# One zero-filled product for the edge values of two query tiles, and two longer times in the planner of an encoder layer

## The chip, the cores and the metric

The kernel runs on one core of a Trainium2 chip. The metric is the device time of one launch in microseconds, the median of three runs. The profile is of one further execution of the same program.

## The reference

A hybrid encoder layer over 1024 positions of 1024 channels, in float32, with weights drawn at random:

```
h = LN1(alpha*x + 0.5*SwiGLU_a(x))
h = LN2(alpha*h + HybridMixer(h))
h = LN3(alpha*h + 0.5*SwiGLU_b(h))
```

Each SwiGLU has 2752 hidden channels. The mixer projects the input to queries, keys and values of 12 heads, to four Fourier groups and to gates. The part that the change touches most is the attention: three groups of four heads, with dilations 1, 4 and 16. A query at place i of its (strided) sequence attends to the keys from i - 64 to i + 64 of it; the sequence of a residue has 1024, 256 or 64 places. The scores get a relative bias, then softmax; the three groups of a head slot are combined by their softmax denominators.

## The kernel before, in words

**Products.** Nearly all products run on TensorE as three single-pass products of "parts": each operand is split into a rounded high part (a copy on ACT, `split.hi`) and the rest (a subtraction on DVE, `split.lo`). Matrix products are made by a seven-product (Strassen-like) scheme; one such product of a pair of column blocks is a job of 12 matmuls of 512 columns at L495. The attention products are plain float32: scores (L1592), transposition of the probabilities (`pt`, L1637) and values (`pv`, L1653). One float32 matmul stands in the trace as two records.

**Stages in order.** First feed-forward layer ("a"): gate and up products, then down products (tiles `qa...`). Values of all heads (`v`). Then 22 column pairs (u, q, s): each "q" pair is queries and keys of one head, and the attention of that head is put between the pair products that follow. Then the two projections of the mixer, the output product, and the second feed-forward layer ("b"; its down products' tiles are `qb...`). Residual, norms and stores go along.

**What sets the order.** A planner in the program (class `Flow`) simulates the engines while it emits instructions. PE has a fixed list of jobs, and "floats" (the attention products) that are emitted between jobs as soon as the planner believes their inputs are ready. Work of DVE (`V`), ACT (`S`) and GpSimd (`G`) is a node with a cost, its predecessors and a due time; each engine's clock in the plan takes the ready node with the earliest due time. Loads (`Q`) are issued on SP when they come due and when a page is free. A predecessor may carry a wait: `(q, 1.5)` means 1.5 us after the plan's end of `q`. In the plan a load ends 2.5 us after its bytes. What is emitted runs in that order on the chip; there each engine waits, in order, for what an instruction really needs, so a wrong time in the plan shows as an engine that stands.

**Buffers.** 46 pages of 128x1024, 11 halves of 128x512 (`NS2`), 8 PSUM banks. A node takes and gives back pages, halves (`halves=`, `hgives=`) and banks in the plan. `fl.later(n, us, hgives=2)` gives two halves back `us` after node `n`, which is how a plan waits for a store: the store itself is a DMA whose end the plan doesn't know.

**An attention step** (`one`, inside `attention`, L1563). Scores go to a bank; DVE adds the bias into a half `p` (L1606) and takes the maxima (L1616); ACT makes the exponentials (L1621); PE transposes `p` in slices of 128 keys (L1637); ACT copies that to a half `pT` (L1642); PE multiplies the values with it (L1653); ACT copies the result to the page `pv` (L1666 to L1671). Two query tiles are a step. For tiles in the middle of a sequence each has 256 keys, two full slices. At the ends of a sequence a tile has 192 keys: 128, and 64 more. The 64 of the two tiles share one slice: keys of the first tile in its rows 0 to 63, keys of the second in rows 64 to 127. There are 20 such steps, one in each head of group 0 and four in each head of group 1. Their list of products is

```python
where = [(qa, ka, P, 0, 0), (qb_, kb_ + 64, P, 0, 1), (qa, ka + P, 64, 0, 2), (qb_, kb_, 64, 64, 2)]
```

(query tile, first key, keys, first row, slice): two products over 128 keys and two over 64, each tile into a bank of its own. `load_values` (L1530) has loaded the values so that the 64 edge rows of both tiles lie above one another in one 128-row slice of its page, under two keys of the table `vf`.

**Weight parts that are stored early** (`keep_halves`, L1807). The output product's operands are cut into parts well ahead, while the values and the head pairs are computed, and kept in DRAM: a half is loaded, copied (L1820) and subtracted (L1824) into two halves, and these are stored by GpSimd's queue (L338) to `wob..._d` or `wot..._d`. There are 28 such pieces; the two halves are given back 6 us after the store's node.

**Down products** (`ffn`, L657). For each of seven products and eleven steps a page `q...` is loaded by SP with two DMAs (L849) and then split on ACT (L358) and DVE (L363). In stage "b" the last product is done by row tile, and its `qb` weight pages are loaded and split in `load_b4`'s loop. After its hidden columns stage "b" ends a pair with ACT copies `t2`, `t3` (L633), a subtraction `t3b` (L718) and further DVE work.

## Time and profile before

| what | us |
|---|---|
| median of 3 runs | 2058.83 |
| lowest, highest | 2058.13, 2060.5 |
| the profiled execution's own time | 2060.76 |
| its span, first to last instruction | 2059.0 |

| engine | busy us | share | instructions |
|---|---|---|---|
| TensorE, products | 2044.1 | 99% | 9451 |
| VectorE | 1333.7 | 65% | 1890 |
| ScalarE | 886.0 | 43% | 1395 |
| GpSimd | 267.5 | 13% | 464 |

The mean granted clock of TensorE was 0.998 of 2.4 GHz. The DMA engines moved 442 MB, 215 GB/s on average. How to read the trace: PE is the product pipe of TensorE, PEld its weight loads, DVE VectorE, ACT ScalarE, POOL GpSimd, SP the engine that issues most DMAs (a trailing q is an engine's queue). L1653 is a line of the program. Matmuls overlap, so the time from one start to the next is the rate, not the length that stands beside it. "[5.69 <-DMA x]" is idle time before an instruction and what ended it.

### The profile page before, as it was taken

The page shows a single profiled execution, that of the slowest core. Times are in us where ns is not written, and L with a number is a line of the kernel's source. Part 1 is how long each engine was busy: PE and PEld are TensorE (multiplying, and loading weights), DVE is VectorE, ACT ScalarE, POOL GpSimd, SP SyncE. Part 2 cuts the span into 40 slices and gives each one's busy share as a digit, 9 for nine tenths or more (in the row PEclk, how much of TensorE's full clock was granted, in tenths as well). Part 3 has the DMA queues.
Part 4 walks back from the last instruction along what each step waited for, and adds up shares of the span by engine and source line. Part 5 has one row for each costly group of instructions (what it writes and reads, how often), then busy time and mean ns, then how long its engine had stood idle before and what let it go on. Part 6 is the DMA issues. An engine that isn't in the chain of part 4 may idle for free.

```text
span 2059.0 us, 25821 instructions
## 1 busy us (share of the span) xinstructions
PE 2044.1 (99%) x9451; PEld 1701.3 (83%) x9451; DVE 1333.7 (65%) x1890; ACT 886.0 (43%) x1395; POOL 267.5 (13%) x464
## 2 busy tenths in 40 slices
PE   9999999999999999999999999999999999999998
PEld 7888888888888888878888888888888888888886
DVE  7765555577585668555656564687876665575565
ACT  6333333454453324555555443235633333355342
POOL 0122111011001122232122110000011101010000
PEclk9999999999999999999999999999999999999999
DMA  5778875599866558986777669584245433358753
GB/s 205 238 235 259 257 225 157 172 340 404 270 208 186 169 206 270 299 235 191 239 197 192 228 224 347 196 307 174 75 156 182 156 133 128 123 192 292 246 173 104
DMA packets 164144, 442.23 MB, mean 215 GB/s; under 512 B 20370, under 2 KB 42722, under 8 KB 163504
## 3 DMA queue, kind: packets, MB, share of 16 engines
q1 hardware_dynamic: 118928, 288.41, 40.9%
q0 software_dynamic: 45088, 152.16, 24.7%
q8 instruction: 74, 1.21, 0.2%
q14 instruction: 54, 0.44, 0.1%
HBM read 329.63 MB, written 176.91 MB: 246 GB/s over the span
## 4 chain that ended last, share of the span: by engine, by line
PE 96%; DMA 1%; issue 1%; DVE 0%; POOL 0%; ACT 0%; SPq 0%; DVEq 0%; POOLq 0%; ACTq 0%
PE Ab L495 13%; PE Aa L495 13%; PE Aq L495 7%; PE Da L495 6%; PE Db L495 5%; PE As L495 5%; PE Dq L495 3%; PE Xa L864 3%; PE Zb L864 3%; PE Xb L864 3%; PE Za L864 3%; PE pj L2110 2%; PE v L1291 2%; PE Ds L495 2%; PE wA L2199 2%; PE pv L1653 2%
## 5 line engine op out<-in xcount | busy, mean ns | idle before, releaser
L1621 ACT ACTIVATE p<-p,stat 128x192 f32<-128x192 f32 (+2 forms) x96 | 42.2, 441 | 25.6 <-DVE stat L1616 25.3
L338 POOL DMA_DIRECT2D hsaa<-t2a x21 | 12.0, 571 | 315.0 <-DVE t2a L730 296.9
L338 POOL DMA_DIRECT2D n_spill<-y x16 | 9.0, 566 | 297.8 <-DVE y L1061 297.8
L338 POOL DMA_DIRECT2D hsba<-t2b x21 | 11.4, 543 | 273.6 <-DVE t2b L730 273.6
L726 DVE TENSOR_TENSOR t2a<-Da,t2a 128x512 f32<-128x512 f32 x21 | 14.5, 692 | 45.2 <-PE Da L495 45.2
L1653 PEld LDWEIGHTS pv<-pT,v 128*128 128x128 f32 (+1 forms) x320 | 37.4, 189 | 5.2
L1653 PE MATMUL pv<-pT,v 128*128 128x128 f32 (+1 forms) x320 | 40.7, 288 | 0.0
L633 ACT ACTIVATE t2a<-Aa 128x512 f32<-128x512 f32 x21 | 12.6, 600 | 64.9 <-PE Aa L495 64.9
L1411 DVE SCALAR_TENSOR_TENSOR oq<-Dq,b_cols,t2q 128x512 f32<-128x512 f32 x12 | 11.8, 984 | 44.1 <-PE Dq L495 44.1
L1606 DVE SCALAR_TENSOR_TENSOR p<-sc,bias 128x512 f32<-128x512 f32 (+1 forms) x40 | 24.6, 620 | 24.2 <-PE sc L1592 14.4
L633 ACT ACTIVATE t2b<-Ab 128x512 f32<-128x512 f32 x21 | 12.6, 600 | 63.8 <-PE Ab L495 63.8
L726 DVE TENSOR_TENSOR t2b<-Db,t2b 128x512 f32<-128x512 f32 x21 | 14.5, 691 | 39.0 <-PE Db L495 39.0
L1592 PE MATMUL sc<-oq,oq 128*128 128x192 f32 (+2 forms) x192 | 35.4, 331 | 0.0
L718 DVE TENSOR_TENSOR t3a<-Da,t3a 128x512 f32<-128x512 f32 x21 | 14.5, 690 | 29.2 <-PE Da L495 26.7
L1592 PEld LDWEIGHTS sc<-oq,oq 128*128 128x128 f32 x192 | 31.0, 196 | 2.2
L495 PE MATMUL Db<-Zs40h,usb 128*128 128x512 f32 x84 | 29.4, 391 | 1.1 <-DVE t3b L718 1.1
L495 PE MATMUL Db<-Zs41h,usb 128*128 128x512 f32 x84 | 29.3, 389 | 0.0
L495 PE MATMUL Da<-Xs40h,usa 128*128 128x512 f32 x84 | 29.3, 389 | 0.0
L495 PE MATMUL Da<-Xs41h,usa 128*128 128x512 f32 x84 | 29.3, 389 | 0.0
L1411 DVE SCALAR_TENSOR_TENSOR oq<-Dq,b_cols,t3q 128x512 f32<-128x512 f32 x12 | 11.9, 992 | 26.8 <-PE Dq L495 24.6
L718 DVE TENSOR_TENSOR t3b<-Db,t3b 128x512 f32<-128x512 f32 x21 | 14.5, 690 | 21.9 <-PE Db L495 20.4
L1616 DVE TENSOR_REDUCE stat<-p 128x2 f32<-128x384 f32 (+2 forms) x40 | 24.2, 618 | 1.0
(7475 smaller groups left out, 7270.8 us busy)
## 6 DMA issues: line engine op xcount, KB each, us to landing
qa<-hsas SPq DMA_DIRECT2D x43, 256.0 KB, 5.8
qa<-tdat SPq DMA_DIRECT2D x43, 256.0 KB, 5.4
qb<-hsbs SPq DMA_DIRECT2D x43, 256.0 KB, 4.4
ga<-in_ffn_gu_dram SPq DMA_DIRECT2D x21, 512.0 KB, 5.9
ua<-in_ffn_gu_dram SPq DMA_DIRECT2D x21, 512.0 KB, 8.4
gb<-in_ffn_gu_dram SPq DMA_DIRECT2D x21, 512.0 KB, 3.6
ub<-in_ffn_gu_dram SPq DMA_DIRECT2D x21, 512.0 KB, 4.5
qb<-tdbt SPq DMA_DIRECT2D x33, 256.0 KB, 4.8
```

Source lines behind the costliest of these rows:

```text
L338: nc.gpsimd.dma_start(*a, **kw)
L495: nc.tensor.matmul(out, pick(w, a)[:, k * P:(k + 1) * P], self.cols(xn, b, k), start=first and k == 0 and ti == 0, stop=last and k == 3 an ...
L633: nc.scalar.activation(H[c, t], B[c, "B"], AF.Copy)
L718: nc.vector.tensor_sub(H[c, "t3"], B[c, "D"], H[c, "t3"])
L726: nc.vector.tensor_sub(H[c, "t2"], B.pop((c, "D")), H[c, "t2"])
L864: nc.tensor.matmul(bank_, a, b, start=first and ti == 0, stop=last and ti == len(todo) - 1, skip_group_check=True)
L1291: nc.tensor.matmul(ps, X2.cols(f"a{hf + 1}{k // 4 + 1}", a, k % 4)[:, mm * P:(mm + 1) * P], pick(wv, b), start=(k == 0 and ti == 0), stop= ...
L1592: nc.tensor.matmul(sv[:, i, :], qk[0][:, qt * P:(qt + 1) * P], qk[1][:, k0:k0 + w], start=True, stop=True, skip_group_check=True)
L1621: nc.scalar.activation(p3()[:, i, :], p3()[:, i, :], AF.Exp, bias=stats[h][:, k, 0:1], scale=1.0, accum_out=stats[h][:, k, 1:2])
L1653: nc.tensor.matmul(out_of(tiles.index(qt)), env["v"][kc, rows], pt[r0:r0 + rows, sl * P:(sl + 1) * P], start=qt not in seen, stop=last, sk ...
L2110: nc.tensor.matmul(bk[hf], pick(wv, a)[:, k, cc * P:(cc + 1) * P], pick(attn[k], b)[:, hf * 512:(hf + 1) * 512], start=(k == 0 and ti == 0 ...
L2199: nc.tensor.matmul(B["w", bk, m], X4.cols(xn, a, k)[:, m * P:(m + 1) * P], pick(w, b), start=new and k == 0 and ti == 0, stop=k == 3 and t ...
```

## The change

- `load_values`: the two 64-row entries become one entry "edge" for the full 128-row slice.
- `turned`: for steps of 192 keys the shared slice is copied into two slices: rows 0 to 63 into the one of the first tile, rows 64 to 127 into the other's. A new DVE node `blank` clears the other 64 rows of each. `values`: the edge keys of both tiles are one product of 256 columns over 128 rows, half of them zeros; both tiles go to one bank, and the two products over 128 keys add to it. `keep`: one copy of 256 columns in place of two of 128.
- The planner's costs of these nodes follow, and the step takes one bank.
- `keep_halves`: the two halves are given back 10 us after the store's node.
- Down products in both feed-forward layers (and the `qb` weight pages of the last product of "b"): the plan lets a split begin 1.5 us after the plan's end of its load.

```diff
@@ -892,7 +892,7 @@
                 first = p not in (2, 3)
                 J[tag, "d", p, j] = n = job((8 if short(p, j) else 12) * MM, step(p, j, SET[p], first), 4 if first and j == 0 else 0, gives=2)
                 q = Q(n, 0.5, load_step(p, j), [(HN[PROD[p][0], j], 4.0)] + source_nodes(PROD[p][1], j), 44.0, pages=1)
-                split(f"q{tag}{p}{j}", lambda p=p, j=j: D_[p, j], lambda t, p=p, j=j: D_.__setitem__((p, j), t), [q], n,
+                split(f"q{tag}{p}{j}", lambda p=p, j=j: D_[p, j], lambda t, p=p, j=j: D_.__setitem__((p, j), t), [(q, 1.5)], n,
                       34.0, under=(0, 512) if short(p, j) else None)
 
         def last_steps(m, j0, j1):
@@ -930,7 +930,7 @@
                 n = J[tag, "u", 0, 0]
                 deps = [x for j in range(2 * i, min(2 * i + 2, PAIRS)) for x in source_nodes("t4", j)]
                 q = Q(n, 0.5, load_b4(i), deps, 88.0 - 8.0 * i, pages=1)
-                split(f"qb{tag}{i}", lambda i=i: D_["b", i], lambda t, i=i: D_.__setitem__(("b", i), t), [q], n,
+                split(f"qb{tag}{i}", lambda i=i: D_["b", i], lambda t, i=i: D_.__setitem__(("b", i), t), [(q, 1.5)], n,
                       80.0 - 8.0 * i, 512 * min(2, PAIRS - 2 * i), under=(0, 0) if short(4, 2 * i) else None)
             for m in range(4):
                 n = J[tag, "u", m, 0]
@@ -1543,14 +1543,14 @@
             rows(tv[64:128, 7:8], 0, 1, 1, 1)
             for i in range(7):
                 vf[64 + P * i, P] = tv[:, i, :]
-            vf[S0 - 64, 64], vf[0, 64] = tv[0:64, 7, :], tv[64:128, 7, :]
+            vf["edge", 0] = tv[:, 7, :]
         elif g == 1:
             rows(tv[:, 0:4], 4 * 64, 4, 4, 1)
             rows(tv[0:64, 4:8], 4 * 192, 4, 4, 1)
             rows(tv[64:128, 4:8], 0, 4, 4, 1)
             for i in range(4):
                 vf[256 * i + 64, P] = tv[:, i, :]
-                vf[256 * i + 192, 64], vf[256 * i, 64] = tv[0:64, 4 + i, :], tv[64:128, 4 + i, :]
+                vf["edge", 256 * i] = tv[:, 4 + i, :]
         else:
             for b in range(2):
                 rows(tv[64 * b:64 * b + 64], b, 16, 8, 2)
@@ -1636,22 +1636,33 @@
                 for sl, x in enumerate(cuts):
                     nc.tensor.transpose(ps[:, sl * P:(sl + 1) * P], flat[:, x:x + P], ident)
 
+            split_ = w == 192
+
             def turned():
-                st["t"] = half(f"pT{g}{h}{si}")
-                k = len(cuts) * P
-                nc.scalar.activation(st["t"][:, :k], st["tp"][:, :k], AF.Copy)
-            split_ = w == 192
+                st["t"] = t = half(f"pT{g}{h}{si}")
+                k = 2 * P if split_ else len(cuts) * P
+                nc.scalar.activation(t[:, :k], st["tp"][:, :k], AF.Copy)
+                if split_:
+
+                    nc.scalar.activation(t[0:64, 3 * P:], st["tp"][0:64, k:k + P], AF.Copy)
+                    nc.scalar.activation(t[64:P, k:3 * P], st["tp"][64:P, k:k + P], AF.Copy)
+
+            def blank():
+                nc.vector.memset(st["t"][0:64, 2 * P:3 * P], 0.0)
+                nc.vector.memset(st["t"][64:P, 3 * P:], 0.0)
 
             def values():
-
-                st["o"] = bk = [bank(f"pv{g}{h}{si}{i}") for i in range(2 if split_ else 1)]
-                out_of = lambda at: bk[at][:, 0:P] if split_ else bk[0][:, at * P:(at + 1) * P]
+                st["o"] = bk = bank(f"pv{g}{h}{si}")
                 seen = set()
                 pt = st.pop("t")
-                for qt, kc, rows, r0, sl in where:
-                    last = rows == 64 if split_ else sum(x[0] == qt for x in where) == 1 + (qt in seen)
-                    nc.tensor.matmul(out_of(tiles.index(qt)), env["v"][kc, rows], pt[r0:r0 + rows, sl * P:(sl + 1) * P],
-                                     start=qt not in seen, stop=last, skip_group_check=True)
+                if split_:
+                    nc.tensor.matmul(bk[:, :2 * P], env["v"]["edge", kb_], pt[:, 2 * P:], start=True, stop=False,
+                                     skip_group_check=True)
+                for qt, kc, rows, r0, sl in where[:2] if split_ else where:
+                    at = tiles.index(qt) * P
+                    last = split_ or sum(x[0] == qt for x in where) == 1 + (qt in seen)
+                    nc.tensor.matmul(bk[:, at:at + P], env["v"][kc, rows], pt[:, sl * P:(sl + 1) * P],
+                                     start=not split_ and qt not in seen, stop=last, skip_group_check=True)
                     seen.add(qt)
 
             def keep():
@@ -1660,15 +1671,15 @@
                 pv, bk = env["pv"], st.pop("o")
                 q0, q1 = tiles[0], tiles[1]
                 if split_:
-                    for at, qt in enumerate(tiles):
-                        dst = (pv[:, qt * P:(qt + 1) * P] if g == 0 else
-                               pv.rearrange("p (a r) -> p r a", r=4)[:, q0 // 2, at * P:(at + 1) * P])
-                        nc.scalar.activation(dst, bk[at][:, 0:P], AF.Copy)
+                    dst = (pv.rearrange("p (t q) -> p t q", q=P)[:, 0:8:7, :] if g == 0 else
+                           pv.rearrange("p (a r) -> p r a", r=4)[:, q0 // 2, :])
+                    src = bk[:, 0:2 * P].rearrange("p (t q) -> p t q", q=P) if g == 0 else bk[:, 0:2 * P]
+                    nc.scalar.activation(dst, src, AF.Copy)
                 elif g == 0:
-                    nc.scalar.activation(pv[:, q0 * P:(q1 + 1) * P], bk[0][:, :2 * P], AF.Copy)
+                    nc.scalar.activation(pv[:, q0 * P:(q1 + 1) * P], bk[:, :2 * P], AF.Copy)
                 else:
                     dst = pv.rearrange("p (a r) -> p r a", r=16)[:, 2 * q0:2 * q0 + 8, :]
-                    nc.scalar.activation(dst, bk[0].rearrange("p (r a) -> p r a", a=64), AF.Copy)
+                    nc.scalar.activation(dst, bk.rearrange("p (r a) -> p r a", a=64), AF.Copy)
             end = si == len(steps) - 1
             f1 = F(0.2 * n if w == P else 0.37 * n, scores, qk_nodes + [x for x in (last_turn[0], qv, qb) if x], 1,
                    gives=2 if end else 0)
@@ -1679,9 +1690,11 @@
             n3 = S(0.63 * n if w > P else 0.5 * n, exps, [n2], slack=8.0)
             exp_n[h].append(n3)
             f2 = F(0.11 * len(cuts), turn, [n3], 1, hgives=1)
-            n4 = S(0.54, turned, [f2], frees=1, halves=1, slack=8.0)
-            f3 = F(0.22 * len(where), values, [n4], 2 if split_ else 1, hgives=1, gives=1 if end else 0)
-            n5 = S(0.4 * n if w > P else 1.0, keep, [f3], frees=2 if split_ else 1, pages=0 if si else 1, slack=8.0)
+            n4 = S(0.95 if split_ else 0.54, turned, [f2], frees=1, halves=1, slack=8.0)
+            if split_:
+                n4 = V(0.25, blank, [n4], slack=8.0)
+            f3 = F(0.88 if split_ else 0.22 * len(where), values, [n4], 1, hgives=1, gives=1 if end else 0)
+            n5 = S(0.45 if w > P else 1.0, keep, [f3], frees=1, pages=0 if si else 1, slack=8.0)
             done_values.append(n5)
             last_turn[:] = [last_turn[1], f2]
         for si, step in enumerate(steps):
@@ -1830,7 +1843,7 @@
             n = S(0.62, hi, [q], at, 20.0, 6.0, halves=2)
             n = V(0.69, lo, [n], at, 20.0, 5.0, hgives=1)
             nodes.append(G(store, [n]))
-            fl.later(nodes[-1], 6.0, hgives=2)
+            fl.later(nodes[-1], 10.0, hgives=2)
         for i, cs in enumerate((L, R)):
             piece(cs, early[i], i)
 
```

## Rows read from the trace of the kernel before

**Rows 1.** The page: head and part 1 (busy us, share, instructions).

```profile
span 2059.0 us, 25821 instructions
PE 2044.1 (99%) x9451; PEld 1701.3 (83%) x9451; DVE 1333.7 (65%) x1890; ACT 886.0 (43%) x1395; POOL 267.5 (13%) x464
```

**Rows 2.** Waits of PE, whole span (total us, times, longest us).

```profile
PE pt L1637 <- ACT p L1621: 2.8, 1, 2.8
PE Db L495 <- DVE t3b L718: 1.1, 1, 1.1
```

**Rows 3.** Chain of waits, 1800:1850 (start us, us, what, instructions).

```profile
1821.35 2.72 PE Ab L495 x12
```

**Rows 4.** Timeline of PE, 896:912 (start us, us; [idle before <-releaser]).

```profile
899.37 0.39 PE L495 MATMUL Aq<-Ya121h,gq6l 128*128 128x512 f32 x1
902.60 2.45 PE L1637 MATMUL pt<-ident,p 128*128 128x128 f32 x8 [2.84 <-ACT p L1621]
904.84 3.19 PE L1592 MATMUL sc<-oq,oq 128*128 128x256 f32 x8
908.67 0.39 PE L495 MATMUL Aq<-Ys30h,t34q6l 128*128 128x512 f32 x1
```

**Rows 5.** Windows: busy PE, PEld, DVE, ACT, POOL; PEclk; DMA share; GB/s.

```profile
902.50:908.00 5.50, 5.31 (x17) 4.15 (x18) 5.27 (x8) 4.64 (x12) 1.15 (x3) 0.50 0.43 173
```

**Rows 6.** Timeline of DVE, 896:905.

```profile
900.45 0.69 DVE L1606 SCALAR_TENSOR_TENSOR p<-sc,bias 128x512 f32<-128x512 f32 x1 [5.69 <-DMA wot_d<-wot21h]
```

**Rows 7.** Timeline of POOL, 876:905; last row: tile `wot_d`, all its transfers.

```profile
887.39 3.74 POOL L338 DMA_DIRECT2D comb_t<-stat  x5 [1.01 <-issue]
891.72 0.55 POOL L338 DMA_DIRECT2D wot_d<-wot21l  x1
...
DMA to landing us min/median/max: 2.3/6.5/11.0
```

**Rows 8.** Timelines of DVE and PE, 1822:1846.

```profile
1839.66 1.23 DVE L363 TENSOR_TENSOR qb17l<-qb,qb17h 128x1024 fp32r<-128x1024 f32 x1 [3.66 <-DMA qb<-tdbt]
...
1840.00 0.39 PE L495 MATMUL Ab<-Za221h,t34b20l 128*128 128x512 f32 x1
1841.54 0.50 PE L495 MATMUL Db<-Zs40h,usb 128*128 128x512 f32 x1 [1.15 <-DVE t3b L718]
```

**Rows 9.** Window of that stall (columns as in rows 5).

```profile
1829.00:1841.00 12.00, 11.39 (x51) 9.09 (x49) 8.30 (x10) 7.23 (x9) 2.86 (x6) 1.00 1.00 368
```

**Rows 10.** Timeline of PE, a 192-key step; second row: its 64-row records.

```profile
947.24 1.03 PE L1653 MATMUL pv<-pT,v 128*128 128x128 f32 x8
947.78 0.38 PE L1653 MATMUL pv<-pT,v 64*128 64x128 f32 x2
...
948.53 0.40 PE L495 MATMUL Aq<-Ya110l,gq8h 128*128 128x512 f32 x1
```

**Rows 11.** Timeline of PE: full-row values of 128 columns; scores of 256.

```profile
883.36 1.05 PE L1653 MATMUL pv<-pT,v 128*128 128x128 f32 x8
884.48 0.40 PE L495 MATMUL Aq<-Ya220l,t34q5h 128*128 128x512 f32 x1
...
980.11 1.89 PE L1592 MATMUL sc<-oq,oq 128*128 128x256 f32 x8
982.30 0.39 PE L495 MATMUL Aq<-Ya120h,gq9l 128*128 128x512 f32 x1
```

**Rows 12.** ACT's groups by shape, 745:1140; last row: line L770.

```profile
L1666 ACT ACTIVATE pv<-pv 128x128 f32<-128x128 f32 x40 | 11.8, 396 | 7.4 <-PE pv L1653 7.3
L1642 ACT ACTIVATE pT<-pt 128x384 f32<-128x384 f32 x20 | 9.3, 491 | 4.1 <-PE pt L1637 4.1
L1668 ACT ACTIVATE pv<-pv 128x256 f32<-128x256 f32 x12 | 4.6, 384 | 8.5 <-PE pv L1653 8.5
...
L770 DVE MEMSET tlsb<- x2: 485/485/485, 1818.0 to 1823.4; 64x512 f32 x2
```

**Rows 13.** Window: first 90 us of attention (columns as in rows 5).

```profile
815.00:905.00 90.00, 87.07 (x451) 73.00 (x450) 51.23 (x71) 53.35 (x126) 25.40 (x43) 0.98 0.93 283
```
## The prediction, made before the changed kernel ran

> **What bounds the kernel now.** I read the page first: TensorE is busy in 2044.1 of 2059.0 us [rows 1]. Busy PE is no proof of PE at its peak, so I next asked what PE waited for. The list has only two waits outside the first 17 us, and both are in stages that the diff touches [rows 2]. The chain of waits gives the rate of a PE that lacks nothing: twelve products of 512 columns take 2.72 us, 0.227 each [rows 3]. Every other view is held against that rate.
>
> The first stall is dearer than its 2.84 us. The last product before it began at 899.37, so the next was due at 899.60; eight records of a transposition and eight of scores follow, then two of the pair products, and the third of those begins at 908.67 [rows 4]. That is 9.07 us. At full speed they need 8 x 0.112 + 8 x 0.217 + 2 x 0.227 = 3.1 us, by the record lengths of [rows 11] ((884.48 - 883.36 - 0.227) / 8 for 128 columns, (982.30 - 980.11 - 2 x 0.227) / 8 for 256). So it costs **6.0 us**: half is standing still, and half is a granted clock of 0.50, the 1.2 GHz level, in the 5.5 us after it [rows 5].
>
> Its cause: DVE's bias addition waited 5.69 us on a store of weight halves [rows 6]; exponentials on ACT, and PE's transpositions, queued behind it. The tile `p` is a buffer of the 11 halves whose earlier owner was still being stored. The store was issued at 891.72, behind a run of gathers on POOL that began at 887.39 [rows 7], and DVE got on at 900.4, some 8 us later; the plan counts 6 us from that issue. Over all transfers of that buffer, nearly all of them such stores, landing took 2.3 to 11.0 us, median 6.5 [rows 7]: 6 is too early for about half, and one of them hit PE.
>
> The second stall: a down-product split on DVE (`qb17l`) waited 3.66 us on a transfer, the subtraction `t3b` stood behind it, and PE's `Db` behind that: due at 1840.23, begun at 1841.54 [rows 8]. **1.3 us**; DMA was full in those 12 us [rows 9].
>
> **The change, part by part.**
>
> *Edge values.* Twenty attention steps have 192 keys (one in each head of the first group, four in each of the second). Today each has two products over 128 keys and two over 64. One of them began at 947.24, its 64-row records at 947.78, the second pair product after it at 948.53 [rows 10], so it costs 948.53 - 947.24 - 0.227 = 1.06 us. Four products over 128 keys cost 884.48 - 883.36 - 0.227 = 0.89 [rows 11]. Afterwards a step is one product of 256 columns over 128 rows (half of them zeros) and two of 128 columns, each in two records: 2 x 0.217 + 4 x 0.112 = 0.88. Saved: 0.18 a step, 20 steps, **3.7 us**, directly on PE, which is the bound.
>
> Two 64-row records stand under one start, 947.78 [rows 10]: they do run side by side, but not for nothing. Four full records at 0.112 from 947.24 are through at 947.69, 0.09 before that start; two pairs at 0.112 would then be through at 948.00, and the pair products are at their rate only from 948.30 (948.53 - 0.227). The Trainium skill, TensorEngine Tiling (Array Packing), "Theoretical Speedup", says that contractions of up to 64 rows run up to twice as fast when tiled, which speaks against this change: by it the step would cost 0.45 + 0.22 = 0.67 us now and 0.88 afterwards, 4.2 us lost over 20 steps. The measured 1.06 decides; the same page's "Key Properties" says that a switch of mode drains the engine, which is where the trace's gaps stand. Bounds for this term: at worst the gaps stay and what ran side by side is paid in full, 1.06 + 0.22 a step, 4.4 us lost; at best 3.7 gained. I take 3.7, since each record length in it is measured at its own width.
>
> ACT, per step: the copy of 384 columns (0.491) becomes one of 256 (0.384) and two of 64x128; two copies out of 128x128 (0.396 each) become one of 256 columns [rows 12]. With 0.4 for a small copy and 0.384 to 0.6 for the last (it is strided in the second group) that is 1.28 before, 1.57 to 1.78 after: up to 0.5 more, 10 us over the stage. DVE gets two clears of 64x128, between 0.12 (a quarter of the 0.485 of 64x512 [rows 12]) and 0.4 each: under 16 us. Both engines are busy for under 60% of that stage [rows 13], so I cost this at nothing; it only makes the values ready about a microsecond later, and PE fills that with pair products that wait for nothing. If that cover is gone (a step becoming due when no pair product is ready) each such place costs its idle time, and the clock if it lasts like the first stall. One PSUM bank less per step can only help. No DMA is added: the edge rows already lie in one page.
>
> *Halves held longer.* The plan frees each pair of stored halves after 10 us where it took 6. Nothing executed changes; the planner puts users of halves later, or does other work first. There are 28 pieces (seven operands, two parts, two column halves), due two jobs apart, 54 jobs from first to last, at least 147 us at 2.72 each [rows 3]. 28 x 2 halves x 4 us over that is at most 1.5 of 11 halves more in use. 10 covers the 8 us of the stall, and all but the slowest landings. I take the whole **6.0 us** as gained; bounds: 0 (another late store takes its place) and 6.0. What is queued behind a lack of halves: `t2` and `t3` copies on ACT, which the next pair product needs.
>
> *Splits later.* The plan now gives each down-product load 1.5 us more before ACT and DVE take its split; the loads themselves and their SP issues keep their due times, but the page is held that much longer; a load that lacks a page would come 1.5 us later, against splits that are due 34 us ahead of their product. In stage "a" no PE stall is there to cure. In "b" `t3b` should pass ahead of the late split. Not certain, since the row names a transfer and not which one: 0 to 1.3, I take half, **0.7 us**.
>
> Sum: 3.7 + 6.0 + 0.7 = 10.4 us off. The profiled execution took 2060.76 (2059.0 span and 1.8 around it), so 2050.4 on its own scale; it was the slowest of those shown, 1.9 above the median of 2058.83. On the median: **2048.4 us**. All three edits also rewrite the planner's whole order from the first down products on, which the sum can't show.
>
> **The rivals.**
> A new wait of the first stall's kind: stores still land up to 11 us after issue, POOL is still held by gathers, so a half handed out after 10 us can be late again. For it: [rows 7]. Against: of the 56 stores (28 pieces, two each) only one held PE up with 6 us. Price 6.0, so 2054.4.
> Lack of halves, the slower side: with 1.5 fewer halves the `t2`/`t3` copies come late in some heads, pair products have nothing to run, and PE idles into the 1.2 GHz level. Each episode costs about 6.0 as the old one did; the gains are 10.4, so the sign turns with the second, and with three (18.0) the time is 2066.4. Against: the waits of PE name no `t2` or `t3` copy of that stage now, and ACT and DVE have 40% of it free [rows 13].
> The overlap rule (as a mechanism of this kernel; the Trainium skill's page is named above): the two-by-two running of 64-row records is lost and the drains stay. Step 1.06 plus the 0.22 that ran hidden: 4.4 lost in place of 3.7 gained, 2056.5. Against: between full-row records there is no such gap [rows 11].
> The change does not do what it says: the stalls stay or move unchanged, and only 3.7 is gained: 2055.1.
>
> **How the numbers follow.** About 0.2% (4.1 us) is what a measurement of this kernel can tell from no change. Chances: the forecast with small remnants 0.60 (faster); one new wait 0.15, whose 2054.4 lies on the bound of 2054.7, so half faster, half the same; stalls unchanged 0.08, the overlap rule 0.04, one or two episodes of lacking halves 0.04, all three the same; three or more episodes 0.09, slower. Faster 0.68, same 0.23, slower 0.09. The range runs from 2046 (the whole second stall gained, and a little of the profiled execution's slack) to 2058, which takes in one new wait, unchanged stalls and the overlap rule; what is left out is mainly lack of halves.
>
> **What would show it.** In the changed profile: the 192-key steps at 0.88 us from first record to the next pair product, with no 64-row records; no PE wait on the exponentials and granted clock 1.00 throughout 815 to 1140 us; no `Db` wait near 1840; ACT and DVE some microseconds busier in the attention stage. I am wrong if the steps still cost 1.06, if a stretch at 0.50 stands anywhere behind a `p`, `t2` or `t3`, or if PE's list has a wait in those stages as long as those there now [rows 2].

## The result, and the profile after

The changed kernel takes **2064.36 us** (median of 11 runs, 2060.61 to 2068.43), the kernel before in the same comparison 2058.97 (2056.11 to 2061.46): ratio **1.0028**, 95% interval 1.0019 to 1.0037. It is 5.4 us slower; 10.4 us less was forecast. The profiled execution after lies on its median, that of before 1.8 us above its own, so a difference read between the two traces flatters the change by 1.8.

Head and part 1 of the page after, beside [rows 1]:

```profile
span 2062.6 us, 25812 instructions
PE 2042.9 (99%) x9411; PEld 1701.7 (83%) x9411; DVE 1340.1 (65%) x1930; ACT 890.0 (43%) x1415; POOL 267.1 (13%) x464
```

PE has 40 records fewer and is 1.2 us less busy, yet the span is 3.6 longer. So PE stands more; and it runs slower in places, since the edge steps alone should have taken 3.7 off its busy time. The list of PE's waits after, without those of the first microseconds (total us, times, longest us), beside [rows 2]:

```profile
PE pt L1637 <- ACT p L1621: 6.3, 2, 3.6
PE pv L1659 <- DVE pT L1652: 2.0, 1, 2.0
...
PE pv L1659 <- ACT t12q5h L358: 0.8, 1, 0.8
```

Where the forecast saw none there are four, and the one at `Db` is gone. The timeline of PE shows them, with the edge step between (start us, us; in brackets the idle time before and what ended it):

```profile
820.16 0.39 PE L495 MATMUL Aq<-Ya121h,gq3l 128*128 128x512 f32 x1
824.11 2.17 PE L1637 MATMUL pt<-ident,p 128*128 128x128 f32 x8 [3.57 <-ACT p L1621]
...
828.70 0.40 PE L495 MATMUL Aq<-Ys30h,t34q3l 128*128 128x512 f32 x1
...
863.39 0.39 PE L495 MATMUL Aq<-Ya221h,t34q4l 128*128 128x512 f32 x1
864.58 0.67 PE L1659 MATMUL pv<-pT,v 128*128 128x256 f32 x2 [0.80 <-ACT t12q5h L358]
...
905.16 0.39 PE L495 MATMUL Aq<-Ya121h,gq6l 128*128 128x512 f32 x1
908.28 0.93 PE L1637 MATMUL pt<-ident,p 128*128 128x128 f32 x4 [2.73 <-ACT p L1621]
...
912.92 0.40 PE L495 MATMUL Aq<-Ys31h,t34q6h 128*128 128x512 f32 x1
...
942.19 0.59 PE L1659 MATMUL pv<-pT,v 128*128 128x256 f32 x2
942.62 0.61 PE L1664 MATMUL pv<-pT,v 128*128 128x128 f32 x4
943.07 0.60 PE L1659 MATMUL pv<-pT,v 128*128 128x256 f32 x2
...
1106.69 0.39 PE L495 MATMUL Aq<-Ya221h,t34q13l 128*128 128x512 f32 x1
1109.11 0.67 PE L1659 MATMUL pv<-pT,v 128*128 128x256 f32 x2 [2.03 <-DVE pT L1652]
```

The edge step is as forecast: 943.07 - 942.19 = 0.88 us, where [rows 10] gave 1.06. The price of each stall is worked out as for [rows 4]:

- **S1, at 820.** Due at 820.39; from there the 8 + 8 records and two pair products need 3.1 us at full speed, and the third pair product begins at 828.70: 8.31 - 3.1 = **5.2 us**.
- **S2, at 863.** Due at 863.62, begun at 864.58: **1.0 us**.
- **S3, at 905.** Due at 905.39. Four transpositions, four scores of 256 and six pair products need 4 x 0.112 + 4 x 0.217 + 6 x 0.227 = 2.7, and the next begins at 912.92: 7.53 - 2.7 = **4.8 us**.
- **S4, at 1107.** Due at 1106.92, begun at 1109.11: **2.2 us**.

Together 13.2 us lost; the old stall's 6.0 and the edge steps' 3.7 gained: +3.5. By the starts of the same instructions in both traces the attention stage lost 4.8 us (0.45 us ahead of before at 780 us, 4.30 behind at 1150); the rest lies in shares of about 0.1 us at the borders between attention products and pair products, which stand elsewhere now.

Two of the stalls carry a lower granted clock, as the old one did [rows 5] (windows; columns as there):

```profile
824.00:828.00 4.00, 3.89 (x15) 2.98 (x16) 0.22 (x1) 4.00 (x12) 0.00 (x0) 0.58 0.38 136
908.00:914.00 6.00, 5.67 (x19) 4.43 (x20) 4.88 (x14) 3.49 (x12) 0.65 (x2) 0.72 0.90 284
```

What stood ahead of each is in the timelines of ACT, POOL and DVE after:

```profile
821.52 0.63 ACT L609 ACTIVATE usq<-uq 128x512 fp32r<-128x512 f32 x1 [4.79 <-DMA uf_d<-uf]
822.16 1.28 ACT L1621 ACT_TABLE_LOAD   x1
823.46 0.51 ACT L1621 ACTIVATE p<-p,stat 128x256 f32<-128x256 f32 x1
...
808.70 0.54 POOL L338 DMA_DIRECT2D uf_d<-uf  x1 [1.61 <-DVE uf L1481]
...
895.82 0.54 POOL L338 DMA_DIRECT2D wot_d<-wot21l  x1 [1.84 <-DMA tdbt<-in_ffn_down_dram]
...
905.52 0.69 DVE L1837 TENSOR_TENSOR wot41l<-wot41r,wot41h 128x512 fp32r<-128x512 f32 x1 [5.15 <-DMA wot_d<-wot21l]
906.13 0.68 DVE L1606 SCALAR_TENSOR_TENSOR p<-sc,bias 128x512 f32<-128x512 f32 x1
...
1106.24 1.23 DVE L1074 TENSOR_TENSOR n<-n,ln1g 128x1024 f32<-128x1024 f32 x1 [1.88 <-DMA n<-n_spill]
1107.38 1.22 DVE L363 TENSOR_TENSOR t12s14l<-t12s,t12s14h 128x1024 fp32r<-128x1024 f32 x1
1108.57 0.17 DVE L1651 MEMSET pT<- 64x128 f32 x1
1108.80 0.17 DVE L1652 MEMSET pT<- 64x128 f32 x1
```

S1 starts in a part of the program that the diff doesn't touch. Each of four Fourier groups has a page `uf`, which GpSimd's queue stores to `uf_d` (issued at L1483); the plan gives the page back 5 us after its node (`fl.later(n, 5.0, gives=1)`, L1487). The last of these stores was issued at 808.70; ACT's `usq` had been given that page and waited for the store until 821.5, nearly 13 us after the issue. The exponentials stood behind it, PE behind them. In S3 DVE's `wot41l` waited until 905.5 for a store of halves that was issued at 895.82, 9.7 us earlier; the new hold of 10 us is counted from the node in the plan. In S4 the value step's copies were ready, but its two clears stood on DVE behind a wait for a load and a split of 1.2 us. S2 has the same form: ACT's half `wot11h` had waited 3.96 us on a store, the copies came behind it, and the clears ended at 864.37.

The late landing of the Fourier pages is not new. From the trace of **before**: the one wait on such a page, and how long all transfers of the tile took to land (four stores, and four loads that read the pages back from 1254 us on):

```profile
795.40 1.23 DVE L363 TENSOR_TENSOR t34q2l<-t34q,t34q2h 128x1024 fp32r<-128x1024 f32 x1 [3.17 <-DMA uf_d<-uf]
...
DMA to landing us min/median/max: 2.9/12.7/15.0
```

And **after**, who waited, and the landings:

```profile
  ACT usq L609: 4.8, 1
  DVE t34q2l L363: 1.4, 1
...
DMA to landing us min/median/max: 3.0/11.8/13.1
```

The stores by themselves landed 2.9, 9.6 and 15.0 us after their issue before (the third of the four has no record), and 3.0, 10.0, 3.0 and 12.8 after; the plan counts 5. Before, a split on DVE waited for the second of them, and PE didn't feel it. Nobody waited for the last and slowest, issued at 808.19 and landed at 823.14: `usq` of that place began at 817.07 without a wait, so it had another page. The new order dealt the page of the last store to `usq`, ahead of exponentials that PE needed at once.

### The profile page after: what moved, and what is told of

Its sections match the earlier page's. It is cut to its first block, busy times and chain, and to the rows that moved or that the text cites. A ratio compares the mean times of both kernels' runs of the same rounds, so it can differ in the third digit from the quotient of the medians.

```text
span 2062.6 us, 25812 instructions
## 1 busy us (share of the span) xinstructions
PE 2042.9 (99%) x9411; PEld 1701.7 (83%) x9411; DVE 1340.1 (65%) x1930; ACT 890.0 (43%) x1415; POOL 267.1 (13%) x464
## 5 line engine op out<-in xcount | busy, mean ns | idle before, releaser
L1664 PEld LDWEIGHTS pv<-pT,v 128*128 128x128 f32 x240 | 32.2, 191 | 2.2
L1664 PE MATMUL pv<-pT,v 128*128 128x128 f32 x240 | 32.4, 274 | 0.0
L1637 PE MATMUL pt<-ident,p 128*128 128x128 f32 x140 | 22.4, 285 | 6.4 <-ACT p L1621 6.3
L1637 PEld LDWEIGHTS pt<-ident,p 128*128 128x128 f32 x140 | 16.9, 144 | 10.5 <-ACT p L1621 8.5
```

The costliest lines, as they stand in the source:

```text
L1637: nc.tensor.transpose(ps[:, sl * P:(sl + 1) * P], flat[:, x:x + P], ident)
L1664: nc.tensor.matmul(bk[:, at:at + P], env["v"][kc, rows], pt[:, sl * P:(sl + 1) * P], start=not split_ and qt not in seen, stop=last, skip_ ...
```

## The experiments

All ran with the kernel before on the same chip; "before" below is its median there. Lines are those of the changed kernel. Values are medians.

**The three parts alone.** Longer hold, without the other two:

```diff
-            fl.later(nodes[-1], 6.0, hgives=2)
+            fl.later(nodes[-1], 10.0, hgives=2)
```

> Only the 10 us hold of the stored weight halves is put into the kernel before. If the longer hold is what costs (halves run short), this alone is slower by 4 to 7 us, with PE waits behind tiles that lack a half. If the order is merely dealt anew, it lies within 4 us of before, with the stall at 901 us moved or of another size and no waits named for a lack of halves. If the clear of the edge halves is the cause, it is 0 to 6 us faster.

Measured: 2061.58 us (before 2058.81), ratio 1.0015 (1.0006 to 1.0024). The stall at 901 is gone, and S1 stands at 820, with the same cause. From the timelines of ACT and PE:

```profile
822.59 0.63 ACT L609 ACTIVATE usq<-uq 128x512 fp32r<-128x512 f32 x1 [5.67 <-DMA uf_d<-uf]
...
825.19 2.17 PE L1637 MATMUL pt<-ident,p 128*128 128x128 f32 x8 [4.44 <-ACT p L1621]
```

So S1 comes with the hold, without any edge product or clear. Priced as above (due 820.59, the third pair product at 829.69) it costs 6.0 us, as much as the stall that went, and the span is only 0.5 longer than that of before (2059.5). The medians differ by 2.8 because the profiled execution of before lies 2 us above its median here and this one on its own. Whether the old stall costs 6.0 in an ordinary execution is not shown.

Later splits, without the other two (and the like in `load_step`, L895):

```diff
-                split(f"qb{tag}{i}", lambda i=i: D_["b", i], lambda t, i=i: D_.__setitem__(("b", i), t), [q], n,
+                split(f"qb{tag}{i}", lambda i=i: D_["b", i], lambda t, i=i: D_.__setitem__(("b", i), t), [(q, 1.5)], n,
```

> Only the 1.5 us for the splits of the down products. All theories: 0 to 1.4 us faster, by the wait of Db near 1840 us. If the order is dealt anew by any edit, the attention stage changes too, by up to 4 us either way; otherwise the stall at 901 us stays at 6.0 us.

Measured: 2058.97 (before 2058.81), ratio 1.0003 (0.9994 to 1.0012). The wait at `Db` is 0.72 us instead of 1.15, with `t3b` still right behind the split `qb17l`; the stall at 901 is untouched (3.15 us of waiting). No difference that can be measured.

Edge product, hold 6 and splits as before:

```diff
-            fl.later(nodes[-1], 10.0, hgives=2)
+            fl.later(nodes[-1], 6.0, hgives=2)
...
-                split(f"qb{tag}{i}", lambda i=i: D_["b", i], lambda t, i=i: D_.__setitem__(("b", i), t), [(q, 1.5)], n,
+                split(f"qb{tag}{i}", lambda i=i: D_["b", i], lambda t, i=i: D_.__setitem__(("b", i), t), [q], n,
```

> Only the edge product. On PE itself 20 x 0.18 = 3.7 us are gained in every theory. If the longer hold is the cause of the loss, this is 3 to 5 us faster than before. If the clear on DVE between the copy and the values is the cause, it gains at most 1.5 us and PE waits at least once for the clear. If the order is dealt anew, the old stall may be gone or another there: anything from 8 us faster to 2 us slower, told by the list of PE waits and not by the part.

Measured: **2054.76** (2053.72 to 2056.41; before 2058.81), ratio 0.9982 (0.9973 to 0.9991). PE's waits, whole list of that stage:

```profile
PE pt L1637 <- ACT p L1621: 1.9, 2, 1.6
...
PE pv L1659 <- DVE pT L1652: 1.0, 1, 1.0
```

The old stall has shrunk by itself: 1.6 us of waiting at 899 and 0.3 behind it, and 2.6 us lost in place of 6.0; the granted clock stayed at 1.00 from 898 to 906. One wait for the clears has come, 1.2 us lost. So the 4.1 us are not the product's alone; a cleaner measure of it comes below.

The same with the clears put ahead, right behind the maxima, long before PE needs them (hold and splits as before):

```diff
-            n4 = S(0.95 if split_ else 0.54, turned, [f2], frees=1, halves=1, slack=8.0)
-            if split_:
-                n4 = V(0.25, blank, [n4], slack=8.0)
+            nb = [V(0.25, blank, [n2], halves=1, slack=8.0)] if split_ else []
+            n4 = S(0.95 if split_ else 0.54, turned, [f2] + nb, frees=1, halves=0 if split_ else 1, slack=8.0)
```

> The edge product with the clear put ahead: the half is taken and its two 64-row quarters are cleared right after the maxima, so that the values wait for ACT's copies alone. If the clear behind the copy costs, this is 2 us faster than edge_only and no PE wait names the clear. If the order is dealt anew, the clear is named nowhere, and the rest differs from edge_only by other stalls of up to 6 us.

Measured: 2054.99 (before 2058.81), ratio 0.9983 (0.9974 to 0.9992). No wait of PE names a clear any more. In time it is the same as the version above, where 2 us were expected: a single wait of 1.2 us is below what the runs can tell.

**Pairs of parts.** Edge product and later splits (hold 6):

```diff
-            fl.later(nodes[-1], 10.0, hgives=2)
+            fl.later(nodes[-1], 6.0, hgives=2)
```

> The changed kernel with the hold back at 6 us (edge product and later splits stay). If the hold costs, this is close to the edge product alone: 2053 to 2056.5 us. If the loss comes from the splits together with the edge product, it stays near 2060 or above.

Measured: 2055.46 (before 2058.40), ratio 0.9983 (0.9975 to 0.9992).

Edge product and hold 10, splits as before (and the like at L895):

```diff
-                split(f"qb{tag}{i}", lambda i=i: D_["b", i], lambda t, i=i: D_.__setitem__(("b", i), t), [(q, 1.5)], n,
+                split(f"qb{tag}{i}", lambda i=i: D_["b", i], lambda t, i=i: D_.__setitem__(("b", i), t), [q], n,
```

> The changed kernel with the splits as before (edge product and 10 us hold stay). If the hold and the edge product cost more together than the sum of each alone (2057.5 by addition), this is near the changed kernel, 2061 to 2066 us, with the waits at 820 and 905 us. If the splits are needed for the loss, it is near 2057.5.

Measured: 2063.77 (2058.00 to 2068.82; before 2058.40), ratio 1.0028 (1.0015 to 1.0040). The whole loss is in this pair. Apart, the edge product gives -4.1 and the hold +2.8, which would be -1.3; together they give +5.4, though with runs 10.8 us apart. (The profile was of its fastest run, 2058.0, and shows S1 with 4.1 us of waiting and no loss at 905, so that trace can't speak for the median.)

Edge product and a hold of 8:

```diff
-            fl.later(nodes[-1], 6.0, hgives=2)
+            fl.later(nodes[-1], 8.0, hgives=2)
```

> Edge product with a hold of 8 us, splits as before. If the cost grows with the hold, because halves get scarce, it lies between the edge product alone (2054.8) and the one with 10 us. If each hold only deals another order, it may lie outside of both, and its PE waits are at other places or absent.

Measured: 2057.07 (before 2058.40), ratio 0.9996 (0.9987 to 1.0005). The time lies between those of 6 and 10, as it would if halves got scarce; but the wait is another: `usq` waits 3.8 us on `uf_d`, PE 2.6 behind it. S1 again, with a smaller change of the number.

**The late page, by the plan.** The changed kernel, with the Fourier page given back after 15 us, the slowest landing seen:

```diff
-        fl.later(n, 5.0, gives=1)
+        fl.later(n, 15.0, gives=1)
```

> The changed kernel, where the plan hands out the page of a Fourier channel block 15 us after its store and not 5. If the stall at 820 us is ACT waiting for that page (its store takes 12.8 us to land), it goes: about 5 us faster than the changed kernel, some 2059 us, with the waits at 863, 905 and 1107 us left. If lack of halves is what holds up the exponentials, the stall stays.

Measured: 2056.70 (before 2058.40), ratio 0.9995 (0.9986 to 1.0004): **about 7 us faster** than the changed kernel (-1.7 against +5.4, each to before), by one number in a line that the change doesn't touch. That is more than the 5 expected, for S1 is gone, and in the neighbourhood of S3 PE has one wait left, of 1.4 us and for other exponentials, until 910.7 (ACT's `wot40h` ahead of them waited 1.3 on a store of halves); a clear is waited for at 1098, 1.8 us.

The kernel before with hold 10 and that number:

```diff
-            fl.later(nodes[-1], 6.0, hgives=2)
+            fl.later(nodes[-1], 10.0, hgives=2)
...
-        fl.later(n, 5.0, gives=1)
+        fl.later(n, 15.0, gives=1)
```

> The kernel before with the 10 us hold and with the page of a Fourier channel block handed out 15 us after its store. If the hold does cure the stall at 901 us (6.0 us) and only uncovered the late page at 820 us, this is 5 to 6 us faster than before, near 2053. If the hold is bad in itself, for lack of halves, it is no faster than before. If orders are dealt anew without a rule, a new wait elsewhere gives back up to 6 us.

Measured: 2055.54 (before 2058.53), ratio 0.9986 (0.9977 to 0.9995); no wait of PE over 0.5 us in the stage. Here the longer hold does what it was meant to, for 3.0 us where 5 to 6 were expected. Stores still land late: bias additions on DVE wait 2.3 us at 857.6 and 2.8 at 897.5 for stores of halves, but PE doesn't feel it there.

All parts, the clears ahead, and that number (to the changed kernel, the two diffs of the clears and of the Fourier page):

```diff
-        fl.later(n, 5.0, gives=1)
+        fl.later(n, 15.0, gives=1)
...
+            nb = [V(0.25, blank, [n2], halves=1, slack=8.0)] if split_ else []
```

> The changed kernel with both mendings: the later page, and the clear ahead of the copy. Against the changed kernel with the later page alone (2056.7) the wait for the clear near 1098 us goes, 1.9 us: 2054 to 2055. If the clear is not what costs there, it stays at 2056.7.

Measured: **2051.16** (2051.03 to 2052.07, 5 runs; before 2058.53), ratio **0.9962** (0.9949 to 0.9976), the fastest version of all, where 2054 to 2055 was expected. PE's waits and the window of the stage:

```profile
PE pv L1667 <- ACT pT L1646: 0.5, 1, 0.5
PE Db L495 <- DVE t3b L718: 0.3, 1, 0.3
```

```profile
815.00:1140.00 325.00, 324.49 (x1676) 277.57 (x1675) 199.33 (x322) 188.29 (x451) 77.12 (x127) 1.00 0.79 236
```

PE is busy in 324.49 of 325 us at full clock; by the starts of the same instructions the stage is 8.5 us shorter than before. That is what the forecast summed up for it (3.7 + 6.0), less 1.2.

The same without later splits, at three holds: 10, 6 and 14. The last of them, against a hold of 10:

```diff
-            fl.later(nodes[-1], 10.0, hgives=2)
+            fl.later(nodes[-1], 14.0, hgives=2)
```

> The best version so far (edge product with the clear ahead of the turned probabilities, half pages held 10 us, the Fourier block's pages given back after 15 us) without the later splits of the down product. If the later splits are worth what the stall at Db in the trace of before was (0 to 1.3 us): 2051.2 to 2052.5. Rival (the re-dealt order of the last stage decides, either way): 2053 to 2055.

> Edge product with the clear ahead, the later page, and the hold of before (6 us). The later page has no PE wait to cure at 6 us of hold, so: 2055 as without it, if only named waits count; if any edit deals the order anew, up to 4 us to either side.

> As the last, with a hold of 14 us. If a hold that covers the landing of nearly all stores takes the waits on them away and halves are not scarce, 2050 to 2053. If halves are scarce by now, slower than 2055, with PE waits behind copies that lack a half.

Measured: hold 10 2052.56 (before 2059.31), ratio 0.9967 (0.9955 to 0.9979), not to be told from all parts. Hold 6: 2056.56 (before 2058.53), 0.9987 (0.9978 to 0.9996); waits for exponentials are back near 900. Hold 14: 2057.13 (before 2058.53), 0.9990 (0.9981 to 0.9999), where 2050 to 2053 was expected if late stores were all; PE waits 1.4 us for a `t3q` copy until 859.8 and 1.2 for exponentials until 928.0. From the timelines of ACT and DVE with hold 14:

```profile
857.66 0.38 ACT L1646 ACTIVATE pT<-pt 128x256 f32<-128x256 f32 x1 [5.35 <-DMA wot_d<-wot30l]
...
857.65 0.17 DVE L1654 MEMSET pT<- 64x128 f32 x1 [5.78 <-DMA wot_d<-wot30l]
```

So a longer hold is no cure either: it counts from the plan's node, the order is dealt anew, and another store comes late (this one landed 11.1 us after its issue). 10 with the Fourier number happens to be an order in which PE feels no late store; that is luck, since nothing in the plan looks for it.

Hold 10 without later splits also measures the edge product by itself. Against before it gives -6.8, and the hold of 10 with the Fourier number alone gives -3.0. The 3.8 us between them are the edge product with its clears ahead, and neither trace has a wait of PE over 0.5 us in the attention stage; the order of instructions differs too, so the 3.8 are not free of its small shares.

**Which stall belongs to what, in one order.** The runs above change the order of instructions whenever they take a part out. The next three leave every engine's order as it is in the changed kernel; what they leave out changes the numbers that are computed. First without the clears:

```diff
-                    nc.scalar.activation(t[0:64, 3 * P:], st["tp"][0:64, k:k + P], AF.Copy)
-                    nc.scalar.activation(t[64:P, k:3 * P], st["tp"][64:P, k:k + P], AF.Copy)
+                    nc.scalar.activation(t[:, 3 * P:], st["tp"][:, k:k + P], AF.Copy)
+                    nc.scalar.activation(t[:, k:3 * P], st["tp"][:, k:k + P], AF.Copy)
...
-                nc.vector.memset(st["t"][0:64, 2 * P:3 * P], 0.0)
-                nc.vector.memset(st["t"][64:P, 3 * P:], 0.0)
+                pass
```

> The changed kernel without its 40 clears; both slices of the turned probabilities are copied from all 128 rows. It leaves out the masking of the edge product; the instructions of every engine keep their order otherwise. Theory (three new stalls of different cause): the wait of a value step for the clear at 1109 us (2.03 us in the trace of the changed kernel) and the part of the wait at 864 us behind it (0.8) are gone, the stalls at 824 us (late store of the Fourier block) and at 905 us (late half page) stay: 2061 to 2062.5. Rival (the 40 clears on DVE, 6.6 us of busy time, delay the whole DVE queue and so cause the stalls at 824 and 905 too): those go as well, 2051 to 2055.

Then without the stores of the Fourier pages (their cost in the plan is kept, and the later loads read another tensor):

```diff
-            uf_d[gi] = kb.dram([P, 1024], f"uf_d{gi}")
-            pool_dma(uf_d[gi], uf)
+            fl.queued(0.57, 4e-6 * P * 1024)
...
-            nc.sync.dma_start(t, uf_d[gi])
+            nc.sync.dma_start(t, xt[0, 0, :, 0:1024])
```

> The changed kernel without the store of the Fourier block's four pages; they are loaded again from the transposed input instead, so the Fourier products are of other numbers. The plan and the order of all other instructions stay. Theory: ACT's half usq has its page without waiting and the stall at 824 us (some 5.2 us of the stage) is gone: 2058.5 to 2060 if the stall at 905 us is of its own cause, 2054 to 2055.5 if that one only follows from the shift. Rival (the re-dealt order loses time at 820 whatever store is late): 2062 to 2064.5.

And both:

> Both edits together, the order of all other instructions that of the changed kernel. It leaves out the masking and the store of the Fourier block. Theory: 2056 if the two add and the stall at 905 us stays, 2051 to 2053 if it goes too (what is then left is the gain of the edge product and of the old stall at 901 us). Rival (the changed order of instructions by itself costs time, in ways that neither wait explains): 2058 or more.

Measured, before 2059.31 in all three: without clears 2061.88 (2057.45 to 2067.53), ratio 1.0017 (1.0007 to 1.0026); without the store 2057.92 (2055.35 to 2063.05), 1.0000 (0.9991 to 1.0009); with neither **2053.16** (2051.93 to 2056.87), 0.9973 (0.9962 to 0.9984). Against before that is +2.6, -1.4 and -6.2, where the changed kernel has +5.4: the clears are worth 2.8 us, the store 6.8, both 11.6. The 2.8 is hardly clear of noise by itself (the intervals of the two ratios overlap); without the store the clears are worth 4.8 (-1.4 against -6.2), and there the intervals lie apart. PE's waits without clears:

```profile
PE pt L1637 <- ACT p L1621: 5.7, 2, 3.5
```

S2 and S4 are gone, S1 and S3 are not: the first theory, and not the rival by which 40 clears hold up all of DVE. PE's waits without the store, and its timeline at the transposition of S3 and the value step of S4 (the order is the same, the times are earlier):

```profile
PE pv L1658 <- DVE pT L1651: 3.4, 1, 3.4
PE Db L495 <- DVE t3b L718: 1.7, 1, 1.7
```

```profile
899.62 0.39 PE L495 MATMUL Aq<-Ya121h,gq6l 128*128 128x512 f32 x1
899.99 0.93 PE L1636 MATMUL pt<-ident,p 128*128 128x128 f32 x4
...
1096.55 0.39 PE L495 MATMUL Aq<-Ya221h,t34q13l 128*128 128x512 f32 x1
1100.37 0.67 PE L1658 MATMUL pv<-pT,v 128*128 128x256 f32 x2 [3.43 <-DVE pT L1651]
```

S1 is gone, and **S3 with it**: the transposition comes 0.37 us behind the product before it, and `wot41l` (897.22 there) no longer waits on a store. So S3 goes with the store that made S1. The last Fourier store is issued some 90 us ahead of S3, so the shift by S1 is the likely link (behind it the work meets the stores of halves at another moment); that link is argued, the rest shown. In exchange S4 grew to 3.6 us: the load ahead of its clears on DVE was waited for 3.3 us there, 1.9 in the changed kernel. The expected 2054 to 2055.5 was missed by just that, and by `Db`.

That `Db` waits 1.65 us here settles the third part. The timeline of DVE without the store, then that of the changed kernel:

```profile
1835.72 1.23 DVE L363 TENSOR_TENSOR qb17l<-qb,qb17h 128x1024 fp32r<-128x1024 f32 x1 [4.16 <-DMA qb<-hsbs]
1836.86 0.69 DVE L718 TENSOR_TENSOR t3b<-Db,t3b 128x512 f32<-128x512 f32 x1
```

```profile
1842.86 1.23 DVE L363 TENSOR_TENSOR qb17l<-qb,qb17h 128x1024 fp32r<-128x1024 f32 x1 [2.56 <-DMA hsbs<-sab]
1844.00 0.68 DVE L718 TENSOR_TENSOR t3b<-Db,t3b 128x512 f32<-128x512 f32 x1
```

In both, `t3b` still stands right behind the late split. The changed kernel only waited less for that transfer.

With neither clears nor store, one wait over 0.5 us is left, 1.16 us for an ACT copy at 1102. The attention stage is 5.9 us shorter than before, of the 9.7 summed up: 1.3 of the 3.8 missing are that wait, 0.9 a slower border at 820; the rest is not settled.

## Why the prediction was wrong, step by step

**Edge values, 3.7 us: right.** 0.88 us a step, no 64-row records, and 3.8 us by the runs that show it without stalls. The -4.1 of the product alone agrees with 3.7 partly by luck: the old stall shrank there and a wait for a clear came. By the estimate from the Trainium skill (TensorEngine Tiling (Array Packing), "Theoretical Speedup") the product with zeros should have lost; a step with the pair of short products and their gaps took 1.06 and one with zeros 0.88, so here the measurement decides, and the rival built on that rule falls.

**"I cost this at nothing": the first step that failed.** The busy time was sized right (a clear is 0.165 us, 40 of them 6.6; ACT grew by 4.0 in all). But the named cover, "PE fills that with pair products that wait for nothing", exists only in the plan. On the chip PE's order is already written: at 1106.69 the next pair products stood behind the value step, and PE stood for a clear that itself stood behind two other instructions of DVE. What was added was not 0.3 us of work but one more hop, through another engine's queue, on a chain that PE waits for. Price: 3.2 us in the trace (S2 and S4), 2.8 by the run without clears, 4.8 where the Fourier stores are gone.

**Halves, 6.0 us: the second step that failed, and the dearer.** A hold of 10 does end the old stall, so the mechanism is right as far as it goes; where no other stall takes its place (hold 10 with the Fourier number) it is worth 3.0 us by the runs. The 6.0 was read from one execution, 1.9 us above its median. The edge product alone, by its other order, had already brought the same stall to 2.6, so on top of it the hold had only that to cure, and whatever its own order brought had to be paid from it. "All three edits also rewrite the planner's whole order from the first down products on, which the sum can't show" was written, and then the sum priced it at nothing: the new order gave the page of another late store to an instruction ahead of PE's work (S1, 5.2 us in the trace; 6.8 by the run without the Fourier stores, with S3). The best version has 8.5 of the 9.7 us of the stage, but nothing in these parts makes it come out so.

The first rival had the kind of wait and nearly its price (5.2 and 4.8, against 6.0), but looked for its source in the halves' own landings [rows 7] and allowed one. S1's source is a page with 5 us in the plan and 12.8 on the chip. S3's is a store of halves, as the rival said, but that stall goes when the Fourier stores go. The landings in the trace of before were to be had for every buffer, and the forecast misread the one it used: [rows 7] is not nearly all stores, for 16 of the 44 transfers with a landing are later loads, and the 11.0 is one of them. The 28 stores alone took 2.3 to 9.4 us, median 6.0, and the one that held DVE up was `wot21h`, issued at 891.12 and landed 9.2 us later, not some 8. So 10 looked safe by that trace; in the changed kernel 10 of all 56 stores of halves took longer than 10 us, where before one of 49 did.

**Later splits, 0.7 us: not shown.** "`t3b` should pass ahead of the late split" is false, by three traces in which it still stands behind it (of the splits alone, the changed kernel, and that without the Fourier stores); alone the part changes nothing that the runs can tell.

**The slower side.** The lack of halves gave 2066.4, close to 2064.4, but it is not what happened: no wait of PE in the changed kernel names a `t2` or `t3` copy, and the loss goes with the clears and the store. The test that the forecast set itself (a stretch near 0.50 behind a `p`, a wait as long as those of [rows 2]) is what the trace shows.

## What to carry to other kernels

In a kernel whose order is written by a plan, a changed number re-deals buffers and places everywhere: before summing gains, list each time that the plan assumes for a transfer beside what the trace says it takes, and treat every one that is too short as a stall that only lacks an instruction ahead of the busiest engine to wait for it. An added instruction is cheap by its length and dear by its queue: put it where its inputs come earliest, not in the middle of the chain. And run the parts alone and in pairs; here two parts that were worth -4.1 and +2.8 made +5.4, and with the Fourier page and the clears mended they made -6.8.

## What the runs showed that was not expected

The clock doesn't follow the length of the standing still alone. After waits of 3.57 and 2.73 us the granted clock fell (0.58 and 0.72 in the windows above); after 2.84 us it was 0.50 [rows 5]. After 3.43 us in the run without the store it did not:

```profile
1100.30:1106.00 5.70, 5.63 (x27) 4.79 (x28) 4.90 (x6) 2.08 (x3) 1.64 (x3) 1.00 0.56 203
```

Ahead of each of these waits PE ran the same 512-column pair products. Behind the three that fell stood transpositions and scores, behind this one a value step and then pair products again. Which of these matters was not tried.

The versions also scatter differently: the changed kernel over 7.8 us and edge product with hold 10 over 10.8, but the edge product alone over 2.7, and all parts with the clears and the Fourier page mended over 1.0 (5 runs). Late stores alone don't explain it: the hold alone, with S1, scatters over 3.2, and the changed kernel without the Fourier stores over 7.7. What it hangs on is not shown.
